# A one-core decoder layer: the first expert pair's token rows are picked by products that hold the one-hot matrix still

## The chip, the cores and the metric

The kernel runs on one core of a Trainium2 chip. The metric is the device time of one execution in microseconds (us). Engines are named as in the profile: PE (TensorE matmul), PEld (its weight load), DVE (VectorE), ACT (ScalarE), POOL (GpSimd) and SP (SyncE, which here only issues DMAs).

## The reference, cut to what matters

One decoder layer on 512 tokens of width 1024 in float32: a token mixer with three branches, then a two-level mixture of experts, then a final RMSNorm. Only the experts matter here. A router gives each token two of 32 experts; each expert is a gated MLP of width 256:

```python
xb = x_pad[toks]                                       # rows of the tokens of one expert
a = jax.nn.silu(xb @ w_gate_e[e]) * (xb @ w_up_e[e])
return a @ w_down_e[e]                                 # then scaled and summed back by token
```

## The kernel before, in words

**Pairs.** The 32 experts are taken as 16 pairs. A pair works on 128 slots, 64 for each of its two experts. Slot-to-token assignment is a one-hot matrix `P` of 512 tokens by 128 slots (`onehot`, L1069, on DVE). `by_slot` (L1074) multiplies it with a few columns on PE, which gives each slot's token number; `place` (L1080, DVE) makes it an index; `fetch` (L1085) issues an indirect gather of 128 rows of 1024 from the copy `xd` in HBM into `self.XG`, on POOL's queue. There are two such buffers: `XG[0]` for even pairs and `XG[1]`, which is a part of the tile `XB`, for odd ones (L995). `turn_x(c)` (L1099) transposes four 128-column blocks of the gathered rows on PE and scales them on ACT. `up(k)` (L1126, `U0` to `U7` in the orders below) multiplies them with one block of gate and up weights for both experts, `turn` (L1137) transposes the result, `down` (L1144, `D`) multiplies it with the down weights. The first nine pairs scatter their result with an accumulating indirect DMA into `xo` in HBM; from then on `xo` is loaded into SBUF (`ACC<-xo`, L1341) and the later pairs are added there by one-hot products (`combine`, L1170).

**The first pair** has no gathered rows. `pick_x(k)` (L1090, `X0` to `X7`) makes the already transposed block k directly: four products over the token tiles, with a block of the token rows `ACC` held in the array and `P` moving.

**Weights.** Each pair has 12 pieces of 512 KB (`w_e`), loaded by SP in a fixed order into a ring of 40 places (L661 to L701). A piece is requested when the piece that held its place before has been multiplied; `used(n)` after every second `up` and after `down` moves that on. SP issues in order: a request whose place isn't free holds back all requests behind it. Pieces 36 to 39 go to the place of `ACC`, the token rows that `pick_x` reads. They are not loaded by `used` but by the step `L` of the order.

**Order.** All engines follow an order that is written out by hand, for pair 0 `SEQ0` (L1276), for the others `SEQM`. `b1` and `b2` are the fetches for pairs 1 and 2, `j` the slot numbers and weights (`info`), `o` a later pair's one-hot matrix, `x0` and `x1` the next pair's `turn_x`, `f` a fetch.

Of the kernel before, what the change touches and what calls it, by code (L numbers as in the profile page):

```python
# [9 lines left out]
F32 = mybir.dt.float32  # L10
# [3 lines left out]
AF = mybir.ActivationFunctionType  # L14
# [23 lines left out]
P_MIX, P_MEM, P_Q, P_KV, P_PS, P_GB, P_FFN, P_END = 0, 8, 16, 19, 21, 25, 49, 57  # L38
# [3 lines left out]
def trunk_and_moe(ctx, tc, a, out):  # L42
    nc = tc.nc
    v, s, g, pe = nc.vector, nc.scalar, nc.gpsimd, nc.tensor
# [34 lines left out]
    def nm(b):  # L79
        n[0] += 1  # L80
        return f"{b}{n[0]}"

    def at(dt=F32, shape=(128, 512)):
        return UA.tile(list(shape), dt, tag="u", name=nm("u"), bufs=8)
# [17 lines left out]
    def mt(dt=F32, shape=(128, 512)):  # L102
        return G2.tile(list(shape), dt, tag="m", name=nm("m"), bufs=6)
# [4 lines left out]
    def bank(p, tag, bufs, shape=(128, 512)):  # L108
        return p.tile(list(shape), F32, tag=tag, name=nm(tag), bufs=bufs)

    def mmb():
        return bank(PA, "mm", 4)

    K = cst.tile([128, C_END], F32, name="K")
    PR = cst.tile([128, P_END], F32, name="PR")
# [223 lines left out]
    ps = mmb()  # L339
# [157 lines left out]
    for h_ in range(XHEADS):  # L497
# [3 lines left out]
        ps = mmb()  # L501
        mm3(ps[:, :MEM], kterms(w, ms))
        tick()
        t = mt()
# [28 lines left out]
    for h_ in range(XHEADS):  # L533
# [22 lines left out]
        ps = mmb()  # L556
        hs = slice(h_ * 128, (h_ + 1) * 128)
# [25 lines left out]
    def swap(src):  # L583
        b = mt()
        for q in range(4):
            o = (q ^ 1) * 32
            s.copy(b[q * 32:(q + 1) * 32], src[o:o + 32])
        return b
# [8 lines left out]
    b = swap(kr)  # L597
# [13 lines left out]
    scale = 192.0 ** -0.5  # L611
# [23 lines left out]
    for d in range(KD):  # L635
        w = WS.use("w_bpm", d)
        res = []
        for j, y in enumerate((yp, ym)):
            ps = mmb()
# [39 lines left out]
    def load_piece(i):  # L679
        e, c = pieces[i]  # L680
        ts = place(i)
        n_ = 2 // len(ts)
        for t in ts:
            if len(ts) == 2:
                t = t.unsqueeze(1)
            sync.dma_start(t, a["w_e"][e, :, c * T:(c + n_) * T].rearrange("p (k f) -> p k f", f=T))
            W[e][c:c + n_] = [t[:, j] for j in range(n_)]
            c += n_
# [12 lines left out]
    def used(n_):  # L701
        ring["used"] += n_
        load(max(min(ring["used"] + RING, 3 * RING - 4), ring["used"] + RING - 4))
# [96 lines left out]
    for h_ in range(HEADS):  # L800
        for op in SEQ:
            k, i = op[0], op[1:]
# [21 lines left out]
            elif k == "V" and h_ % 2:  # L824
                p = (h_ + 1) // 2
# [97 lines left out]
    def row_major():  # L923
        return W1.tile([128, 8, T], F32, tag="ac", name=nm("ACC"), bufs=1).rearrange("p (t a) b -> p t (a b)", t=4).rearrange("p t (a b) -> p t a b", b=128)

    ACC = row_major()
# [65 lines left out]
    def ct2(dt=F32):  # L992
        return C2.tile([128, 1024], dt, tag="y", name=nm("y"), bufs=3)

    XG = [ct2(), XB[:, 0:2].rearrange("p a b -> p (a b)")]  # L995
    g.memset(XG[0], 0.0)
    RR, sm = ct2(), ct2()
    R1, R2 = (RR[:, i * 512:i * 512 + 512].rearrange("p (a b) -> p a b", a=4) for i in range(2))
    L = R1[:, :, 0:36]
# [4 lines left out]
    def bc(x, *shape):  # L1004
        while len(x.shape) < len(shape):
            x = x.unsqueeze(len(x.shape))
        return x.broadcast_to(list(shape))
# [31 lines left out]
    tokr = cst.tile([128, 4, 2], F32R, name="tokr")  # L1039
# [12 lines left out]
    PC = Scope("pc", space=PSUM).p  # L1052
# [8 lines left out]
    def ut(shape, dt=F32):  # L1061
        return W1.tile(list(shape), dt, tag="e1", name=nm("u"), bufs=18) if extra[0] else at(dt, shape)

    class Pair:
# [22 lines left out]
            g.indirect_dma_start(out=self.XG, out_offset=None, in_=xd[:, :], in_offset=bass.IndirectOffsetOnAxis(ap=ix[:, :1], axis=0),  # L1087
                                 bounds_check=T - 1, oob_is_err=False)

        def pick_x(self, k):  # L1090

            if k % 4 == 0:
                self.xps = bank(PC, "xe", 2, (128, 4, 128))
                self.xe.append(ut((128, 4, 128)))
            for t in range(4):
                pe.matmul(self.xps[:, k % 4], lhsT=ACC[:, t, k], rhs=self.P[:, t].bitcast(F32), start=t == 0, stop=t == 3)
            s.activation(self.xe[-1][:, k % 4], self.xps[:, k % 4], AF.Copy, scale=PR[:, P_FFN + k:P_FFN + k + 1])

        def turn_x(self, c):  # L1099
            ps = bank(PC, "xe", 2, (128, 4, 128))  # L1100
# [69 lines left out]
    def combine(i, q):  # L1170
        t, hs = i // 2, slice((i % 2) * 512, (i % 2) * 512 + 512)
        cb = bank(PC, "cb", 1) if i % 2 else bank(PC, "xe", 2)
        for j in range(2):
            pe.matmul(cb, lhsT=q.PT[:, t], rhs=q.y[j][:, hs], start=j == 0, stop=j == 1)  # L1174
        dst = ACC[:, t].rearrange("p a b -> p (a b)")[:, hs]
        v.tensor_tensor(dst, dst, cb, op=OP.add)  # L1176

    def pairs(x):
        return x.rearrange("p t (b a) -> p t a b", b=2)
# [5 lines left out]
    PP = [Pair(p, pairs(code)[:, :, p], None, scattered=p < SC) for p in range(NP)]  # L1185
    for q in PP[:3]:
        q.onehot()


    v.tensor_reduce(sm[:, 6], t4, axis=AX, op=OP.add)  # L1190
    v.scalar_tensor_tensor(sm[:, 9], sm[:, 8], 1.0, sm[:, 6], op0=OP.add, op1=OP.mult)
# [3 lines left out]
    v.tensor_tensor(t32, A1, bc(sm[:, 10], 128, 4, 32), op=OP.mult)  # L1195
    v.tensor_tensor(Wd, A2, bc(sm[:, 11], 128, 4, 32), op=OP.mult)
    v.tensor_tensor(Wd, Wd, t32, op=OP.add)
    tok = K[:, C_TOKID:C_TOKID + 4]
    INF = cst.tile([128, 4, NE // 2, 8], F32R, name="INF")

# [9 lines left out]
    def tiles():  # L1210
        mps = bank(PC, "y", 2, (128, 32))
        for t in range(4):
            pe.matmul(mps, lhsT=KB[:, B_ONES:B_ONES + 128], rhs=Ab[:, t], start=t == 0, stop=t == 3)
        v.reduce_max(nt[:, 0:16], mps.rearrange("p (b a) -> p a b", b=2), axis=AX)
        v.reduce_max(nt[:, 16:17], nt[:, 0:16], axis=AX)
        v.tensor_scalar(flag, nt[:, 16:17], float(CAP), None, op0=OP.is_gt)
# [56 lines left out]

    SEQ0 = "X0 b1 X1 b2 X2 U0 X3 U1 X4 U2 X5 U3 X6 U4 X7 U5 j0 o U6 j1 x0 U7 L x1 j2 j f".split()  # L1276
    SEQM = "o U0 c U1 j c U2 c t c U3 x0 D n U4 w c U5 c x1 c U6 f c U7".split()
    SEQL = "t D U0 U1 U2 U3 U4 U5 U6 U7".split()
    todo = []
# [2 lines left out]
    def wide():  # L1282
        return W0.tile([128, 2, T], F32, tag="e0", name=nm("e"), bufs=6).rearrange("p a b -> p (a b)")

    for p, q in enumerate(PP):
        q.wts = [W[2 * p], W[2 * p + 1]]
        last = p == NP - 1
        if p == NP - 2:
            gf = XG[0]
            g.dma_start(gf, a["final_g"].broadcast_to([128, D]))  # L1290
        if last:
            while todo:
                todo.pop(0)()
            order.__exit__(None, None, None)
            with tc.If(nc.values_load(flag[0:1, 0:1], min_val=0, max_val=1) > 0):
                extra[0] = True
                overflow()
                extra[0] = False
            order = tc.manual_schedule()
            order.__enter__()  # L1300

            q.rw = fs[:, 0, 3:4]
            v.tensor_tensor(q.rw, q.rs, q.wt, op=OP.mult)
        for op in (SEQ0 if p == 0 else SEQL if last else SEQM):
            n_ = int(op[1]) if len(op) > 1 else p + 3
            if op[0] == "U":
                q.up(n_)
                if n_ % 2:
                    used(2)
            elif op == "c" and todo:  # L1310
                todo.pop(0)()
            elif op[0] == "X":
                q.pick_x(n_)
            elif op[0] == "b":
                PP[n_].fetch(PP[n_].by_slot(tokr, 2)[:, 0:1])
            elif op[0] == "x" and not last:
                PP[p + 1].turn_x(n_)
            elif op == "w" and SC <= p < NP - 1:
                q.where()
            elif op == "L":  # L1320
                PP[0].place(PP[0].it[:, 6:7])
                for i in range(RING - 4, RING):
                    load_piece(i)
            elif op == "n" and p == 1:
                tiles()
            elif op[0] in "ojf" and n_ < NP:
                if op[0] == "o":
                    PP[n_].onehot()
                if op[0] == "j":
                    PP[n_].info()  # L1330
                if op[0] == "f":
                    PP[n_].fetch(PP[n_].it[:, 6:7])
            elif op == "t":
                PP[p - 1].turn()
            elif op == "D":
                PP[p - 1].down()
                used(4)
                if p == SC:
                    ACC = row_major()
                    for t in range(4):  # L1340
                        g.dma_start(ACC[:, t].rearrange("p a b -> p (a b)"), xo[t * 128:(t + 1) * 128])  # L1341
                if p > SC:
                    todo += [lambda i=i, q=PP[p - 1]: combine(i, q) for i in range(8)]

    junk, o = wide(), wide()
    hs = [slice(hf * 512, hf * 512 + 512) for hf in range(2)]
    s.activation(fs[:, 4, 0:1], q.a[:, 0:1], AF.Sqrt, scale=0.0)
    ys = [bank(PC, "y", 2) for hf in range(2)]
    for t in range(4):
# [7 lines left out]
        f = fs[:, t]  # L1357
# [9 lines left out]
    f = fs[:, 4]  # L1367
# [103 lines left out]
```

## Time and profile before

| | |
|---|---|
| times of three runs | 804.89, 805.36, 809.42 us (median 805.36) |
| the profiled execution | 807.81 us, of which the span is 806.0 us |
| granted TensorE clock | 0.991 of full speed |
| PE busy | 779.0 us (97%) |
| DVE, ACT, POOL busy | 365.8, 304.4, 276.8 us |
| DMA | 164.17 MB, mean 204 GB/s; weights and other SP and ACT loads 50.3% of the 16 engines' span |

A busy share of PE tells little by itself, since matmuls are pipelined and a slower stream of them still counts as busy. The stage matters: the expert pairs run from 526 us to the end, and there the DMA engines are nearly as full as PE.

### The profile page before, as it was taken

How to read it: one execution, taken by the hardware profiler on the slowest of the kernel's cores; microseconds unless marked ns; L12 is line 12 of the kernel's file. 1: busy time of each engine (PE TensorE's matmuls, PEld its weight loads, DVE VectorE, ACT ScalarE, POOL GpSimd, SP SyncE). 2: the span in 40 equal slices, each digit the busy share in tenths (PEclk: the TensorE clock that was granted, in tenths of full speed). 3: DMA queues.
4: the chain of work that ended last, by engine and by line, in shares of the span. 5: the costliest groups of instructions: out<-in, count | busy, mean ns of one | idle time of the engine just before them, and what ended most of it. 6: DMA issues, size and time to landing. Idle time of an engine off the chain costs nothing. (4 is left out here: it accounts for less than half of the span.)

```text
span 806.0 us, 10157 instructions
## 1 busy us (share of the span) xinstructions
PE 779.0 (97%) x3741; PEld 524.1 (65%) x3743; DVE 365.8 (45%) x675; ACT 304.4 (38%) x626; POOL 276.8 (34%) x169
## 2 busy tenths in 40 slices
PE   7999999999999999999999999999999999999894
PEld 3778888888887888788888888754333333333331
DVE  5668693243455134677774532323121223454424
ACT  6254453343336444655553321213222222222232
POOL 3256677533332688422225644311121212000000
PEclk9999999999999999999999999999999999999988
DMA  6533333321121322111224489979999999999933
GB/s 223 179 105 105 105 105 136 125 105 71 62 92 38 98 95 92 46 47 56 79 87 176 147 313 340 372 257 354 394 370 397 391 374 392 405 354 408 405 125 120
DMA packets 53509, 164.17 MB, mean 204 GB/s; under 512 B 7906, under 2 KB 9058, under 8 KB 53456
## 3 DMA queue, kind: packets, MB, share of 16 engines
q1 hardware_dynamic: 46224, 149.14, 50.3%
q0 software_dynamic: 4640, 9.90, 3.8%
q10 hardware_dynamic: 2592, 4.46, 1.5%
q8 instruction: 30, 0.49, 0.2%
q14 instruction: 23, 0.19, 0.1%
HBM read 158.82 MB, written 11.53 MB: 211 GB/s over the span
## 5 line engine op out<-in xcount | busy, mean ns | idle before, releaser
L125 POOL TENSOR_TENSOR wl<-r,wh 128x1024 fp32r<-128x1024 f32 (+3 forms) x75 | 167.7, 2244 | 210.8 <-ACT wh L180 189.7
L180 ACT CAST wh<-r 128x1024 fp32r<-128x1024 f32 (+3 forms) x85 | 82.1, 972 | 32.0 <-PE mm L199 12.6
L1131 PE MATMUL gu<-e,u 128*64 128x512 f32 x336 | 88.8, 607 | 0.9 <-DMA e<-in_w_e 0.9
L198 PE MATMUL mm<-g,wh 128*128 128x512 f32 x180 | 71.9, 400 | 0.0
L199 PE MATMUL mm<-g,wh 128*128 128x512 f32 x180 | 70.2, 390 | 0.0
L1107 ACT ACTIVATE u<-xe,PR 128x128 f32<-128x128 f32 x120 | 34.2, 367 | 67.4 <-PE xe L1103 67.3
L471 PE MATMUL mm<-box,wh 128*128 128x512 f32 x144 | 56.8, 394 | 0.9 <-ACT wh L180 0.9
L472 PE MATMUL mm<-box,wh 128*128 128x512 f32 x144 | 56.3, 391 | 0.0
L201 PE MATMUL mm<-g,wl 128*128 128x512 f32 x180 | 52.7, 391 | 0.0
L1158 POOL DMA_INDIRECT xo<-y,ix x9 | 14.3, 1594 | 89.9 <-DVE ix L1082 79.7
L435 ACT ACTIVATE m<-s,st 128x256 f32<-128x256 f32 (+3 forms) x48 | 24.3, 508 | 54.4 <-DVE st L433 53.9
L1131 PEld LDWEIGHTS gu<-e,u 128*64 128x64 f32 x336 | 20.4, 135 | 33.0 <-issue 26.1
L1167 PE MATMUL y<-e,u 128*64 128x512 f32 x160 | 38.9, 600 | 0.4 <-DMA e<-in_w_e 0.4
L201 PEld LDWEIGHTS mm<-g,wl 128*128 128x128 f32 x180 | 33.8, 188 | 7.5 <-POOL wl L125 0.2
L198 PEld LDWEIGHTS mm<-g,wh 128*128 128x128 f32 x180 | 34.0, 189 | 6.5
L199 PEld LDWEIGHTS mm<-g,wh 128*128 128x128 f32 x180 | 33.9, 188 | 6.4
L476 PE MATMUL mm<-box,wl 128*128 128x512 f32 x144 | 36.6, 390 | 0.0
L198 PE MATMUL mm<-box,wh 128*128 128x512 f32 x78 | 31.7, 406 | 0.5 <-DVE g L283 0.5
L471 PEld LDWEIGHTS mm<-box,wh 128*128 128x128 f32 x144 | 27.1, 188 | 6.7 <-ACT wh L180 1.3
L1154 DVE TENSOR_SCALAR y<-y,it 128x512 f32<-128x512 f32 x9 | 6.8, 751 | 54.1 <-PE y L1167 54.1
L476 PEld LDWEIGHTS mm<-box,wl 128*128 128x128 f32 x144 | 27.0, 188 | 5.8
L472 PEld LDWEIGHTS mm<-box,wh 128*128 128x128 f32 x144 | 27.1, 188 | 5.3
(358 smaller groups left out, 1657.3 us busy)
## 6 DMA issues: line engine op xcount, KB each, us to landing
e<-in_w_e SPq DMA_DIRECT2D x124, 512.0 KB
r<-in_w_in SPq DMA_DIRECT2D x37, 512.0 KB
r<-in_w_e SPq DMA_DIRECT2D x15, 512.0 KB
wh<-in_w_e SPq DMA_DIRECT2D x15, 512.0 KB
wl<-in_w_e SPq DMA_DIRECT2D x15, 512.0 KB
m<-in_w_e SPq DMA_DIRECT2D x30, 256.0 KB
r<-in_w_bpm SPq DMA_DIRECT2D x8, 512.0 KB
r<-in_w_bl SPq DMA_DIRECT2D x8, 512.0 KB
```

What stands on the lines that cost most here:

```text
L125: eng.tensor_tensor(lo, x, hi.bitcast(F32), op=OP.subtract)
L180: s.copy(hi[:, :cols], r[:, :cols])
L198: pe.matmul(ps, lhsT=lh, rhs=rh, start=start and i == 0, stop=False)
L199: pe.matmul(ps, lhsT=lh, rhs=rl, start=False, stop=False)
L201: pe.matmul(ps, lhsT=ll, rhs=rh, start=False, stop=stop and i == m - 1)
L435: s.activation(P[:, :w], S[:, :w], AF.Exp, bias=st4[:, 0:1], accum_out=st4[:, 1:2])
L471: pe.matmul(ps, lhsT=lh, rhs=rh, start=k == 0, stop=False)
L472: pe.matmul(ps, lhsT=lh, rhs=rl, start=False, stop=False)
L476: pe.matmul(ps, lhsT=ll, rhs=rh, start=False, stop=k == KD - 1)
L1107: s.activation(x[:, j], ps[:, j], AF.Copy, scale=PR[:, k:k + 1])
L1131: pe.matmul(gu[r], lhsT=self.xe[k // 4][:, k % 4, r], rhs=self.wts[b][k], start=k == 0, stop=k == KD - 1)
L1167: pe.matmul(y[r], lhsT=self.aT[:, k, r], rhs=self.wts[b][8 + 2 * k + hf], start=k == 0 and not more, stop=k == 1)
```

## The change

The first pair's rows are no longer made in transposed form. `pick_x(hf)` now holds a tile of the one-hot matrix in the array and moves 512 columns of the token rows, for each half of the width; ACT copies the result into `XG[0]`, and the ordinary `turn_x` transposes it. Both halves stand right behind the first one-hot matrices, ahead of the order `SEQ0`, with pair 1's slot numbers between them. The step `L`, the request for the four pieces in the place of `ACC`, stands behind the first `turn_x` instead of behind `U7`. Pair 0's place index, which stood in `L` too, becomes a step `p` of its own. The fetch for pair 2, which writes `XG[0]`, stands behind `X1`. `XG[0]` is no longer cleared.

```diff
     XG = [ct2(), XB[:, 0:2].rearrange("p a b -> p (a b)")]
-    g.memset(XG[0], 0.0)
...
-        def pick_x(self, k):
-
-            if k % 4 == 0:
-                self.xps = bank(PC, "xe", 2, (128, 4, 128))
-                self.xe.append(ut((128, 4, 128)))
+        def pick_x(self, hf):
+
+            hs = slice(hf * 512, hf * 512 + 512)
+            ps = bank(PC, "y", 2)
             for t in range(4):
-                pe.matmul(self.xps[:, k % 4], lhsT=ACC[:, t, k], rhs=self.P[:, t].bitcast(F32), start=t == 0, stop=t == 3)
-            s.activation(self.xe[-1][:, k % 4], self.xps[:, k % 4], AF.Copy, scale=PR[:, P_FFN + k:P_FFN + k + 1])
+                pe.matmul(ps, lhsT=self.P[:, t].bitcast(F32), rhs=ACC[:, t, 4 * hf:4 * hf + 4].rearrange("p a b -> p (a b)"), start=t == 0, stop=t == 3)
+            s.copy(self.XG[:, hs], ps)
...
+    def first_fetch(p):
+        PP[p].fetch(PP[p].by_slot(tokr, 2)[:, 0:1])
+
+    PP[0].pick_x(0)
+    slot1 = PP[1].by_slot(tokr, 2)
+    PP[0].pick_x(1)
...
     v.tensor_tensor(Wd, Wd, t32, op=OP.add)
+    PP[1].fetch(slot1[:, 0:1])
     tok = K[:, C_TOKID:C_TOKID + 4]
...
-    SEQ0 = "X0 b1 X1 b2 X2 U0 X3 U1 X4 U2 X5 U3 X6 U4 X7 U5 j0 o U6 j1 x0 U7 L x1 j2 j f".split()
+    SEQ0 = "X0 L U0 X1 b2 U1 U2 U3 U4 U5 j0 o U6 j1 x0 U7 p x1 j2 j f".split()
...
             elif op[0] == "X":
-                q.pick_x(n_)
+                q.turn_x(n_)
             elif op[0] == "b":
-                PP[n_].fetch(PP[n_].by_slot(tokr, 2)[:, 0:1])
+                first_fetch(n_)
...
+            elif op == "p":
+                PP[0].place(PP[0].it[:, 6:7])
             elif op == "L":
-                PP[0].place(PP[0].it[:, 6:7])
                 for i in range(RING - 4, RING):
                     load_piece(i)
```

## Rows read from the trace of the kernel before

**Rows 1.** The page's second part: the span in 40 slices of 20.15 us, busy tenths of PE and of the DMA engines, and GB/s.

```profile
PE   7999999999999999999999999999999999999894
...
DMA  6533333321121322111224489979999999999933
GB/s 223 179 105 105 105 105 136 125 105 71 62 92 38 98 95 92 46 47 56 79 87 176 147 313 340 372 257 354 394 370 397 391 374 392 405 354 408 405 125 120
```

**Rows 2.** The busy times by stage: stretch, its length, busy us of PE, PEld, DVE, ACT and POOL with the number of instructions, then granted clock, DMA share and GB/s.

```profile
531.50:534.50 3.00, 3.00 (x18) 1.36 (x16) 0.00 (x0) 0.73 (x2) 1.04 (x1) 1.00 0.55 157
534.50:550.00 15.50, 15.18 (x90) 8.38 (x88) 4.07 (x21) 4.12 (x13) 0.00 (x0) 1.00 0.74 249
550.00:561.00 11.00, 11.00 (x58) 4.01 (x56) 1.77 (x10) 2.94 (x9) 2.61 (x2) 1.00 1.02 373
561.00:594.00 33.00, 32.72 (x158) 11.76 (x156) 6.50 (x22) 9.06 (x27) 6.29 (x5) 1.00 1.03 390
...
700.00:762.50 62.50, 62.07 (x262) 23.01 (x258) 32.17 (x58) 15.80 (x42) 2.54 (x3) 1.00 1.01 391
764.50:771.50 7.00, 6.12 (x16) 1.98 (x18) 0.75 (x1) 1.06 (x2) 0.00 (x0) 0.52 1.00 383
```

**Rows 3.** The waits of SP, the queue that requests the pieces (L686), from 530 to 552 us: who it waited for, us in total, times, longest.

```profile
SPq L686 <- PE gu L1131: 15.3, 5, 5.0
```

**Rows 4.** The same view from 575 to 700 us.

```profile
SPq L686 <- DMA e<-in_w_e: 60.7, 51, 2.2
...
SPq L686 <- PE gu L1131: 2.5, 9, 0.4
```

**Rows 5.** The instructions of PE in order of time, 655 to 705 us. L1140 is a pair's turn, L1167 a down.

```profile
657.26 0.44 PE L1140 MATMUL at<-K,u 128*128 128x128 f32 x2
...
670.43 0.44 PE L1140 MATMUL at<-K,u 128*128 128x128 f32 x2
...
673.66 1.07 PE L1167 MATMUL y<-e,u 128*64 128x512 f32 x2 [0.19 <-DMA e<-in_w_e]
...
682.05 0.73 PE L1174 MATMUL xe<-y,u 128*128 128x512 f32 x2 [0.70 <-DVE ACC L1176]
...
693.63 0.38 PE L1140 MATMUL at<-K,u 128*128 128x128 f32 x2
```

**Rows 6.** The same view, 700 to 806 us.

```profile
712.68 0.38 PE L1140 MATMUL at<-K,u 128*128 128x128 f32 x2
...
730.18 0.38 PE L1140 MATMUL at<-K,u 128*128 128x128 f32 x2
...
781.03 1.98 PE L1356 MATMUL y<-ACC,P 128*128 128x512 f32 x4 [0.60 <-DVE ACC L1176]
```

**Rows 7.** The instructions of PE in order of time, 526 to 549 us (idle time before and its releaser in brackets). L1096 is a pick, L1077 a by_slot, L1131 an up, L1103 a turn_x.

```profile
526.05 1.16 PE L1096 MATMUL xe<-P,ACC 128*128 128x128 f32 x8
526.96 0.58 PE L1077 MATMUL at<-tokr,P 128*128 128x2 f32 x4
...
531.57 1.08 PE L1131 MATMUL gu<-e,u 128*64 128x512 f32 x4
...
533.67 1.08 PE L1131 MATMUL gu<-e,u 128*64 128x512 f32 x4
...
545.08 0.66 PE L1103 MATMUL xe<-K,XB 128*128 128x128 f32 x4
...
548.54 0.65 PE L1131 MATMUL gu<-e,u 128*64 128x512 f32 x2
```

**Rows 8.** All instructions of line L1356, the last pair's product with the one-hot matrix held and the token rows moving: weight loads and passes, ns shortest, median and longest.

```profile
L1356 PEld LDWEIGHTS y<-ACC,P x16: 186/188/190, 781.0 to 791.7; 128*128 128x128 f32 x16
L1356 PE MATMUL y<-ACC,P x16: 592/592/697, 781.0 to 792.1; 128*128 128x512 f32 x16
```

**Rows 9.** Groups of ACT by shape, 505 to 520 us (busy us, mean ns of one), and an ACT row of the order of time.

```profile
L915 ACT COPY ACC<-tr 128x512 f32<-128x512 f32 x2 | 1.2, 585 | 4.7 <-PE tr L911 4.7
...
545.78 1.14 ACT L1107 ACTIVATE u<-xe,PR 128x128 f32<-128x128 f32 x4 [3.24 <-PE xe L1103]
```

**Rows 10.** The gathers: POOL in order of time, 526 to 560 us, and the last line of what the trace says of line L1087 as a whole.

```profile
530.26 1.09 POOL L1087 DMA_INDIRECT XB<-xd,ix  x1 [7.13 <-DVE ix L1082]
531.65 1.04 POOL L1087 DMA_INDIRECT y<-xd,ix  x1 [0.30 <-issue]
...
DMA to landing us min/median/max: 3.3/8.3/15.3
```

**Rows 11.** The instructions of SP in order of time, 527 to 562 us, neighbours merged: start, us from the first's start to the last's end, what, how many.

```profile
534.77 12.80 SPq L686 DMA_DIRECT2D e<-in_w_e  x8
547.80 1.83 SPq L686 DMA_DIRECT2D ac<-in_w_e  x4
```

**Rows 12.** Busy times in stretches of half a microsecond (columns as in rows 2).

```profile
535.00:535.50 0.50, 0.50 (x7) 0.50 (x6) 0.00 (x0) 0.00 (x0) 0.00 (x0) 1.00 0.00 0
535.50:536.00 0.50, 0.50 (x6) 0.34 (x6) 0.00 (x0) 0.13 (x1) 0.00 (x0) 1.00 0.87 123
```

**Rows 13.** The load of the accumulated rows, POOL and DVE in order of time.

```profile
674.10 2.21 POOL L1341 DMA_DIRECT2D ACC<-xo  x4 [8.03 <-DMA e<-in_w_e]
...
681.31 0.69 DVE L1176 TENSOR_TENSOR ACC<-ACC,xe 128x512 f32<-128x512 f32 x1 [1.22 <-DMA ACC<-xo]
```

**Rows 14.** A step of the chain that ended last: start, us, what.

```profile
766.04 6.41 PE y L1167 x16
```

## The prediction

> **What bounds the kernel now.** I read the page's 40 slices first [rows 1]. From slice 24 PE and the DMA engines are both nearly full, except that DMA falls from 372 to 257 GB/s in the slice at 524 to 544 us, the stage of the change. Next the stretches [rows 2]: from 531.5 to 534.5 us DMA moves 157 GB/s, to 550 us 249, then 373, 390 and more at a share of 1.02 to 1.03. So weight pieces come at full rate from 550 us on, with a hole of 18.5 us before. The waits of SP say why. In the hole it waits for PE's ups alone (15.3 us, five times) [rows 3]: each pair of pieces needs a place that two ups free. From 575 to 700 us it waits almost only for earlier DMAs (60.7 us on e alone, 2.5 us on ups) [rows 4].
>
> Who sets the end? A pair without stalls takes PE 13.17 us from turn to turn (657.26 to 670.43), the next one takes 23.2 (to 693.63), with waits for pieces [rows 5]; then 19.05, and 17.5 when nothing stalls and eight combines are in it [rows 6]. The 23.2 us hold seven combines, one of some 0.6 us less, so 16.9 were due: 6.3 us lost, and 1.5 in the next, 7.8 in all. After 700 us PE is busy for 62.07 of 62.5 us [rows 2]. So pieces arrive too slowly for PE until 698 us, PE uses up its lead by 672 us and waits; from there it works without a pause to the end. What DMA delivers earlier before 698 us comes off the end, up to 7.8 us plus what PE gains itself.
>
> **The picks.** Removed are eight picks of 1.16 us each, most of them between ups; a pick and an up together take 2.10 us (531.57 to 533.67) [rows 7]. Added are two half picks, each four float32 products of 512 columns in two passes. The last pair's product has this very shape: one pass lasts 592 ns, a group's first up to 697 [rows 8], and four passes take 1.98 us, so a pass follows the last after (1.98 - 0.70) / 3 = 0.43 us [rows 6]. A half pick is 8 x 0.43 + 0.1 = 3.55 us. The first starts at 526.05 as the pick does now [rows 7] and ends at 529.6, pair 1's by_slot takes 0.5, the second half pick runs from 530.1 to 533.65. ACC is then free.
>
> Each of the 16 loads of the one-hot tile takes 188 ns [rows 8]. Four loads and four passes one behind the other would take L1356 0.75 + 4 x 0.43 + 0.16 = 2.6 us; it took 1.98 [rows 6], so the loads lie beside the passes. [...]
>
> **Turns, copies, small steps.** X0 and X1 are turns of 0.66 us [rows 7]. ACT copies each half in 0.585 us and scales four blocks in 1.14, the first in 0.37 [rows 9]. The copy of the second half stands ahead of X0's scaling: 533.8 to 534.4; U0 starts at 534.9, against 531.57 now. Then X1, b2 and seven ups without picks between (two passes side by side by two, 0.86 us, and some 0.1 where another kind of work stood ahead): U1 ends at 537.8, U3 at 539.5, U5 at 541.3, U7 at 544.6. Pair 1's U0 comes at about 546.8 instead of 548.54 [rows 7]: PE gains 1.7 us.
>
> Pair 1's fetch: its by_slot is done at 530.1, so the gather is issued at about 530.5 against 530.26 [rows 10]. DVE waits there for PE some 1.5 us, and the INF instructions behind it too; their first reader, j0, is at 541, so that is hidden; were it not, 1.5 us. Pair 2's gather moves from 531.65 to about 537.5, with only gathers behind it on POOL; it lands after 8.3 us in the median, 15.3 at worst [rows 10], at 546 to 553, and pair 1's x0 needs it at about 551.6. At worst PE waits a microsecond while it has a lead of tens; nothing. The memset on POOL, the index p and the order on DVE have one answer, nothing.
>
> **The request L.** Now it stands behind U7: four pieces at 547.80, behind eight that trickled out from 534.77 over 12.8 us [rows 11]. After the change SP reaches L first; it needs the place of ACC, free at 533.65. Queued behind it on SP are all further pieces, the first of which needs U1, 537.8, so they lose nothing. Pieces move about 0.75 us after the request: DMA stands still from 535.0 to 535.5 and moves from 535.5 on, after the request at 534.77 [rows 11, 12]. So L moves from 534.5; four pieces of 524 KB at 390 GB/s last 5.4 us, to 539.9. U1 has then freed two more (2.7 us, to 542.6), U3 two (545.3), U5 two (547.9), U7 two (550.6), pair 1's U1 the next at 548.7. The stream doesn't break again.
>
> **The sum.** At 390 GB/s the hole could carry 18.5 x 390 = 7215 KB; it carried 3.0 x 157 + 15.5 x 249 = 4331. Missing are 2884 KB, 7.4 us. What remains is 531.5 to 534.5. If the 471 KB that move there now still do, 1.8 us are missing; if they don't, since pair 2's gather (512 KB) moves out of it into the full stream, 3.0. So DMA is 4.4 to 5.6 us ahead. By shares instead of bytes: (1.03 - 0.55) x 3 + (1.03 - 0.74) x 15.5 = 5.9, 5.8 us at a full share of 1.03, less 3.0: 2.8 us. The share counts a packet that waits as busy and bytes count a small-packet gather as idle; I take 4.0 us, and keep 2.8 and 5.6. Behind 550 us places are freed in time: PE frees them 1.7 us earlier, and some six pieces are on their way by then, 8 us of DMA. PE reaches its starvation 1.7 us earlier, loses 7.8 + 1.7 - 4.0 = 5.5 us instead of 7.8, and everything behind is 4.0 us earlier. Profiled: 807.81 - 4.0 = 803.8 (span 802.0). That execution stood 2.45 us above the median of the runs; from the median 805.36, **801.4 us**.
>
> **Rivals.**
> - *The accumulated rows hold PE.* ACC<-xo is issued at 674.10, behind a scatter that waited 8.03 us, and DVE waits for it at 681.31 [rows 13], PE at 682.05 [rows 5]. It hangs on pair 8's down, which is not starved and gains only PE's 1.7 us. For: the wait exists already. Against: from 682.05 to the turn at 693.63 stand five ups of 0.93, five combines of 0.62 and a by_slot of 0.5, 8.3 us, where 11.6 were spent; 3.3 of the 7.8 us are lost there and 1.5 behind, and can be won there. It would leave 1.7 us: 803.7. Chance 0.14.
> - *Hidden anyway.* The ring's places or the slower gathers give back the gain by 600 us: 805.4. For: SP still waits for ups for 2.5 us between 575 and 700. Against: these waits are of 0.4 us at most, beside 60.7 us for DMAs [rows 4]. Chance 0.10.
> - *More.* The whole hole closes because the first gather fills what remains: 7.4 us, 798.0. The starvation of 7.8 us could carry it. Chance 0.13.
> - *The picks end late.* All of SP's queue stands behind L, so each microsecond that ACC is freed later costs one. It decides at 4 us: L behind 537.7 us is no gain. [...] Chance 0.05.
> - *Loads that aren't hidden.* 16 loads of 0.188 us on the picks' path free ACC at 536.7: a gain of 1.0 us, 804.4. Against: the row of four passes [rows 6]. Chance 0.03. [...]
>
> **How the numbers follow.** The forecast has 0.55, 799.8 to 802.6. The rivals have the rest. The range that leaves out no more than 2 in 10 runs from 798.0 (the end of *more*) to 805.8 (*hidden* with a little noise; the three runs lie 0.5 to 4.5 us apart). One per cent, 8.05 us, is about what a measurement of this kernel can tell from no change, and nearly every case lies inside: 0.05 faster (a part of *more*, with noise), 0.92 within, 0.03 slower (*late*, beyond what is priced).
>
> **What would show it.** In the profile after: two groups of eight passes of about 3.6 us at 526 and 530; four ac pieces requested near 533.7; SP's waits for ups between 530 and 552 down from 15.3 us to few, replaced by waits for DMAs; a DMA share near 1 from 535.5; pair 1's U0 near 546.8; the turns up to the one at 670.43 earlier by 1.7 us, and those from 700 on by 4. It is wrong if ac is requested after 537, if a second hole opens, or if the turns near 690 gain only 1.7 us.

## The result, and the profile after

The changed kernel takes **802.37 us** (median of 20 runs, 800.6 to 804.6); the kernel before, in 20 runs beside them, 807.79 (804.89 to 811.6). The ratio is 0.9931 (0.992 to 0.9943): 5.4 us or 0.7% faster. Forecast were 801.4 us, in 798.0 to 805.8, and a gain of 4.0. The profiled execution took 801.17 us, span 799.4, granted clock 0.995.

The page's slices of 20.0 us first (busy tenths of the DMA engines, GB/s). The slice with the first pair now moves 309 GB/s, 257 before [rows 1]; the two slices don't begin at the same work, so the stretches further below are the better measure.

```profile
DMA  6523334322221323211115479999999999999943
GB/s 218 187 106 106 106 106 132 132 80 80 80 79 44 108 89 82 64 47 57 54 54 211 132 281 339 363 309 392 390 381 388 398 353 399 407 360 403 408 170 121
```

The instructions of PE in order of time, from the first pick on. L1094 is a half pick, L1076 a by_slot, L1101 a turn_x, L1129 an up.

```profile
526.55 3.70 PE L1094 MATMUL y<-ACC,P 128*128 128x512 f32 x8
529.69 0.90 PE L1076 MATMUL at<-tokr,P 128*128 128x2 f32 x4
530.46 3.68 PE L1094 MATMUL y<-ACC,P 128*128 128x512 f32 x8
533.97 0.60 PE L1101 MATMUL xe<-K,y 128*128 128x128 f32 x4
535.08 1.08 PE L1129 MATMUL gu<-e,u 128*64 128x512 f32 x4 [0.51 <-ACT u L1105]
...
546.93 1.94 PE L1129 MATMUL gu<-e,u 128*64 128x512 f32 x8
```

The instructions of SP in order of time, then its waits from 530 to 552 us (us in total, times, longest), then the stretches (columns as in [rows 2]).

```profile
534.20 1.75 SPq L686 DMA_DIRECT2D ac<-in_w_e  x4
538.12 29.37 SPq L686 DMA_DIRECT2D e<-in_w_e  x24
```

```profile
SPq L686 <- PE gu L1129: 11.7, 6, 2.9
SPq L686 <- PE y L1094: 2.8, 1, 2.8
```

```profile
532.00:535.00 3.00, 2.57 (x9) 1.09 (x8) 0.00 (x0) 0.83 (x3) 0.76 (x1) 1.00 0.54 169
535.00:550.50 15.50, 15.10 (x81) 7.05 (x82) 4.78 (x26) 4.61 (x17) 2.03 (x2) 1.00 1.00 360
550.50:561.00 10.50, 10.50 (x54) 3.70 (x55) 1.23 (x5) 3.74 (x11) 2.66 (x2) 1.00 1.03 408
```

The first pair's stage is as the change meant it: two half picks, the four ac pieces requested 13.6 us earlier than in [rows 11], and a DMA share of 1.00 where it was 0.74 [rows 2]. Now follows the place where PE ran out of pieces [rows 5]: rows of PE, POOL and DVE from 662 us on, and all that the trace lists as waits of PE from 650 to 712 us.

```profile
668.82 0.44 PE L1138 MATMUL at<-K,u 128*128 128x128 f32 x2
...
670.79 3.65 PE L1165 MATMUL y<-e,u 128*64 128x512 f32 x16
...
680.48 0.73 PE L1172 MATMUL xe<-y,u 128*128 128x512 f32 x2 [2.41 <-DVE ACC L1174]
...
683.47 2.84 PE L1129 MATMUL gu<-e,u 128*64 128x512 f32 x8
...
687.92 0.61 PE L1076 MATMUL at<-INF,P 128*128 128x8 f32 x4
...
690.61 0.38 PE L1138 MATMUL at<-K,u 128*128 128x128 f32 x2
```

```profile
662.87 1.59 POOL L1156 DMA_INDIRECT xo<-y,ix  x1 [10.19 <-DMA e<-in_w_e]
672.32 2.22 POOL L1348 DMA_DIRECT2D ACC<-xo  x4 [7.86 <-DMA e<-in_w_e]
```

```profile
679.74 0.69 DVE L1174 TENSOR_TENSOR ACC<-ACC,xe 128x512 f32<-128x512 f32 x1 [2.89 <-DMA ACC<-xo]
```

```profile
PE xe L1172 <- DVE ACC L1174: 2.4, 1, 2.4
```

No wait for a piece is listed any more: the down at 670.79 runs in one block, where the one at 673.66 of [rows 5] stopped for its weights. In place of these waits stands one of 2.41 us for the accumulated rows, 0.70 before [rows 5]. Behind it the granted clock falls to 0.50:

```profile
682.00:685.30 3.30, 3.30 (x10) 1.10 (x10) 1.44 (x3) 0.00 (x0) 1.03 (x1) 0.50 1.03 411
```

### The profile page after: what moved, and what is told of

Its sections match the earlier page's. It is cut to its first block, busy times and chain, and to the rows that moved or that the text cites. A ratio compares the mean times of both kernels' runs of the same rounds, so it can differ in the third digit from the quotient of the medians.

```text
span 799.4 us, 10085 instructions
## 1 busy us (share of the span) xinstructions
PE 771.9 (97%) x3703; PEld 520.1 (65%) x3703; DVE 365.8 (46%) x675; ACT 305.0 (38%) x628; POOL 276.1 (35%) x168
## 5 line engine op out<-in xcount | busy, mean ns | idle before, releaser
L1129 PE MATMUL gu<-e,u 128*64 128x512 f32 x336 | 85.6, 613 | 0.5 <-ACT u L1105 0.5
L1105 ACT ACTIVATE u<-xe,PR 128x128 f32<-128x128 f32 x128 | 36.6, 368 | 70.7 <-PE xe L1101 67.3
L1129 PEld LDWEIGHTS gu<-e,u 128*64 128x64 f32 x336 | 20.4, 137 | 33.6 <-issue 30.1
L1165 PE MATMUL y<-e,u 128*64 128x512 f32 x160 | 37.0, 599 | 0.0
```

The lines of the kernel that those rows point to most:

```text
L1105: s.activation(x[:, j], ps[:, j], AF.Copy, scale=PR[:, k:k + 1])
L1129: pe.matmul(gu[r], lhsT=self.xe[k // 4][:, k % 4, r], rhs=self.wts[b][k], start=k == 0, stop=k == KD - 1)
L1165: pe.matmul(y[r], lhsT=self.aT[:, k, r], rhs=self.wts[b][8 + 2 * k + hf], start=k == 0 and not more, stop=k == 1)
```

## The experiments

Absolute times of two executions differ for reasons that have nothing to do with the change: the mixer ends at another time (first picks from 525.65 to 528.48 us in the table below), the full DMA stream is a little faster or slower (352 and 368 GB/s from 650 to 675 us in b0 and in the execution forecast from), the clock falls in the program's last pairs (0.50 from 764.8 to 771.6 us in that execution) or not (1.00 in after). So I read every trace by three lengths worked out from the starts in the order of PE's instructions: **A**, from the first pick to the turn at 670.43 us in [rows 5] (144.38 us there); **B**, from that turn over the next two intervals to the one at 712.68 in [rows 6] (42.25 there; 34.4 without stalls, by the prediction's 16.9 + 17.5, but 35.3 with a term that it left out, see below); **C**, the last interval between two turns. The three intervals between B and C took 52.23 to 52.25 us in every trace.

| kernel | median us | ratio to before | first pick | A | B | C |
|---|---|---|---|---|---|---|
| before, the execution forecast from | 807.79 | | 526.05 | 144.38 | 42.25 | 18.87 |
| b0_before | 806.39 | 0.9978 (0.9955 to 1.0001) | 526.18 | 144.39 | 44.00 | 17.24 |
| b1_before | 809.31 | 1.0023 (0.9997 to 1.0049) | 526.75 | 146.00 | 42.61 | 15.86 |
| e1_request_late | 807.76 | 0.9999 (0.9979 to 1.002) | 526.01 | 142.28 | 44.43 | 18.82 |
| e2_order_alone | 805.82 | 0.9978 (0.9958 to 0.9998) | 526.12 | 145.04 | 41.63 | 17.54 |
| e5_before_less_four | 805.08 | 0.9975 (0.996 to 0.9991) | 525.69 | 144.40 | 40.35 | 17.56 |
| e9_both_before | 804.50 | 0.9968 (0.995 to 0.9987) | 528.13 | 145.97 | 40.03 | 15.85 |
| after | 802.37 | 0.9931 (0.992 to 0.9943) | 526.55 | 142.27 | 40.21 | 15.86 |
| a0_after | 802.33 | 0.9923 (0.9897 to 0.995) | 528.48 | 142.27 | 40.41 | 15.86 |
| e3_combine_late | 801.25 | 0.9918 (0.9886 to 0.995) | 525.65 | 142.27 | 39.81 | 15.86 |
| e4_after_less_four | 802.01 | 0.9938 (0.9915 to 0.9961) | 526.62 | 142.27 | 39.84 | 17.55 |
| e6_split_release | 800.68 | 0.9919 (0.9897 to 0.994) | 526.64 | 142.26 | 40.01 | 17.55 |
| e7_split_and_late | 801.33 | 0.9928 (0.9907 to 0.9949) | 525.68 | 142.26 | 40.34 | 17.55 |
| e8_both_after | 801.78 | 0.9934 (0.9906 to 0.9962) | 528.04 | 142.28 | 39.42 | 15.84 |

The lengths are worked out before the starts are rounded, so they can differ by 0.01 from the rows. Each ratio is to runs of the kernel before on the same chip in the same round, whose medians were 807.72 (a0, e1, e2, e3), 806.96 (e4 to e7), 806.61 (e8, e9) and 807.42 us (b0, b1); between rounds the ratios are to be compared. The kernel before itself came out at 0.9978 and at 1.0023 with eight runs each (b0, b1), so a median that is 0.2% off shows little alone. A is 146 in b1 and e9: in b1 the granted clock stood at 0.50 from 531.5 to 534.5 us, during the picks; that it did so in e9 is inferred from its A alone.

**a0_after** is the changed kernel again, and **b0_before** and **b1_before** the kernel before; their turn comes last.

> The changed kernel again, beside the kernel before on the same chip. Every theory expects the ratio of the first measurement, 0.993 (5.4 us). The theory that the tail's clock is a matter of chance expects the granted clock to differ from run to run between about 0.987 and 0.995, and the runs with the higher clock to be 1.5 to 2 us shorter; if the clock were part of the change, all runs of it would have the higher one.

802.33 us, the same again. From 672 to 698 us, where the wait for the rows stands, PE is idle for 2.83 us. The granted clock differs from run to run as expected: the three runs at 0.992 or more took 800.96 to 801.12 us, the five at 0.991 or less 802.15 to 803.65.

**e1_request_late: the early picks without the early request.**

```diff
-    SEQ0 = "X0 L U0 X1 b2 U1 U2 U3 U4 U5 j0 o U6 j1 x0 U7 p x1 j2 j f".split()
+    SEQ0 = "X0 U0 X1 b2 U1 U2 U3 U4 U5 j0 o U6 j1 x0 U7 L p x1 j2 j f".split()
```

> The changed kernel with the request L back behind U7, nothing else. Theory 'stream' (the gain is that DMA isn't idle before the first ups free places): DMA then stands still from about 534.5 until U1 frees two places at 538.1 and they move at 538.9, 4 us later than now, and nothing behind makes that good; 4 us slower than the changed kernel, about 806.4, level with the kernel before within 1.5 us. Rival 'PE' (the gain is PE's 1.6 us and the denser products): the picks and ups are the same, so the time stays at 802.4.

The whole gain is gone (807.76), within the 1.5 us that the first theory allowed. Stretches, and the wait for a piece that is back:

```profile
535.00:539.00 4.00, 4.00 (x24) 1.83 (x22) 0.16 (x1) 1.41 (x6) 1.03 (x1) 1.00 0.15 23
539.00:550.00 11.00, 10.68 (x60) 5.07 (x56) 4.62 (x25) 2.66 (x9) 0.99 (x1) 1.00 0.98 350
```

```profile
688.59 1.07 PE L1129 MATMUL gu<-e,u 128*64 128x512 f32 x2 [1.45 <-DMA e<-in_w_e]
```

PE is 2.1 us early in A, as in the changed kernel, and B gives 2.2 back. While pieces are late, a faster PE only waits for them sooner.

**e2_order_alone: the early request with the old picks.** All eight old picks stand ahead of the first up, `L` behind them; pair 0's place index is a step `p` of its own here too.

```diff
-    SEQ0 = "X0 b1 X1 b2 X2 U0 X3 U1 X4 U2 X5 U3 X6 U4 X7 U5 j0 o U6 j1 x0 U7 L x1 j2 j f".split()
+    SEQ0 = "X0 b1 X1 X2 X3 X4 X5 X6 X7 L U0 b2 U1 U2 U3 U4 U5 j0 o U6 j1 x0 U7 p x1 j2 j f".split()
```

> The kernel before with its old picks (token rows held, one-hot matrix moving), but all eight picks ahead of U0, the request L right behind X7, and pair 2's fetch behind U0: the order without the new form. Theory 'stream': the picks end at about 526.5 + 8 x 0.97 + 0.5 = 534.8, L is requested at 535.0, 0.8 us behind the changed kernel; U0 follows at once, with no copies and no turn before the ups: 0 to 1 us slower than the changed kernel, 802.5 to 803.5. Rival 'form' (products that hold the one-hot matrix are what gains): no gain, 807 to 808.

A miss for both: 805.82 lies between the two ranges. Picks in a row cost more than picks between ups. PE, then SP:

```profile
529.35 1.16 PE L1096 MATMUL xe<-P,ACC 128*128 128x128 f32 x8 [0.46 <-ACT u L1097]
...
535.09 1.16 PE L1096 MATMUL xe<-P,ACC 128*128 128x128 f32 x8 [0.46 <-ACT u L1097]
536.71 1.16 PE L1096 MATMUL xe<-P,ACC 128*128 128x128 f32 x8 [0.46 <-ACT u L1097]
```

```profile
537.93 1.75 SPq L686 DMA_DIRECT2D ac<-in_w_e  x4
```

A pick comes every 1.62 us (535.09 to 536.71), since most wait 0.46 us for ACT, which scales the block before; between ups that wait was covered (the trace of before lists none ahead of a pick). So `ACC` is free 3.7 us later than in the changed kernel (534.20), and the request, with all of SP's queue behind it, is late by as much. The median is 3.5 us above the changed kernel's, and A and B together are 4.2 us longer than after's, 2.8 of it in A (PE itself is late) and 1.4 in B (the pieces). The sum is near the price that the prediction's fourth rival gave, 1 us for each us that the picks end late, but two thirds of it are PE's own lateness and not the queue's. Against the kernel before, the 1.9 us are not clear of the spread of its own medians (b0 has the same 0.9978), and A + B, 186.67, is that of the execution that I forecast from, 186.63. So the order alone doesn't give the gain: it needs the new form of the picks.

**e4_after_less_four and e5_before_less_four: a faster stream, nothing else.** In both, pieces 36 to 39 aren't loaded; POOL zeroes their place. These four are the whole of pair 2's down weights (two for each of its experts, L657), not half as the expectations say, so pair 2's result is left out of the sum.

```diff
-                    load_piece(i)
+                    e, c = pieces[i]
+                    t = place(i)[0]
+                    g.memset(t, 0.0)
+                    W[e][c:c + 2] = [t[:, 0], t[:, 1]]
```

> The changed kernel without the load of pieces 36 to 39 (half of the down weights of pair 2; their place is set to zero by POOL, so pair 2's result is left out). DMA has 2.1 MB less to move, 5.4 us at 390 GB/s, and is that much further ahead. Theory 'stream, then accumulated rows': the waits for pieces near 690 go, but the wait for the accumulated rows at 680 stays, so only 0.5 to 1.5 us are gained: 801 to 802. If pieces were still all that binds: 5 us, 797.5.

> The kernel before without the load of the same four pieces (the same part is left out). Picks, ups and their order stay as they are. Theory 'stream': 5.4 us less for DMA ahead of the starvation are worth about what the change was, until the wait for the accumulated rows binds: 5 to 6 us faster than the kernel before, 802 to 803. Rival 'PE' (the gain of the change was in the picks and their order): no gain, 807.5.

The changed kernel doesn't mind (802.01, 4.95 us under the kernel before beside it, where a0 was 5.39 under): it isn't pieces that it waits for. The kernel before gains 1.9 us and not 5 to 6, a miss. That median alone is no larger than the spread of b0 and b1, but A + B, 184.74, lies 1.9 us below the lowest of the three traces of before. Its PE, 672 to 698 us:

```profile
672.04 3.65 PE L1167 MATMUL y<-e,u 128*64 128x512 f32 x16
...
681.73 1.07 PE L1174 MATMUL xe<-y,u 128*128 128x512 f32 x2 [2.40 <-DVE ACC L1176]
```

With the pieces out of the way, the accumulated rows hold PE at once, by 2.40 us, as in the changed kernel. B is 40.35, the changed kernel's 40.21; what is left between these two is A, 2.1 us.

**e3_combine_late, e6_split_release, e7_split_and_late, e8_both_after, e9_both_before: what stands behind the rows?** e3 is the changed kernel with the combines of the pair that first reads the rows moved behind more of its ups:

```diff
+    SEQC = "o U0 U1 j U2 t U3 x0 D n U4 w U5 x1 U6 f U7 c c c c".split()
...
-        for op in (SEQ0 if p == 0 else SEQL if last else SEQM):
+        for op in (SEQ0 if p == 0 else SEQL if last else SEQC if p == SC + 1 else SEQM):
```

e6 takes both halves of the picks token tile by token tile, and loads each of the four pieces straight into the part of `ACC` that its tile leaves, so that the first is requested at 531.30. e7 is both edits.

```diff
...
-        def pick_x(self, hf):
+        def pick_x(self, ts):
...
+            for t in ts:
+                if t == 0:
+                    self.xps = [bank(PC, "y", 2) for hf in range(2)]
+                for hf in range(2):
+                    pe.matmul(self.xps[hf], lhsT=self.P[:, t].bitcast(F32), rhs=ACC[:, t, 4 * hf:4 * hf + 4].rearrange("p a b -> p (a b)"), start=t == 0, stop=t == 3)
...
```

> The changed kernel; in pair 10 alone the first four combines stand behind U7 instead of between its ups. In the changed kernel's trace PE waits 2.41 us at 680.5 for DVE, which waits for the load of the accumulated rows, and the granted clock is 0.5 for 3.4 us behind it. Theory 'accumulated rows bind now': the wait and the clock's fall go, 4 us of PE; the pieces become the next bound, and the time falls by 1 to 3 us, to 799.5 to 801.5. Theory 'pieces still bind at pair 10's down': the time falls by less than 1 us. It is slower if the four combines in a row wait for DVE (0.69 us each, about 0.1 us a combine).

> The changed kernel with the picks taken token tile by token tile for both halves at once, and with pieces 36 to 39 loaded into the tile of the token rows itself, so that each of the four is requested as soon as its own token tile has been read: at 528.4 (behind the earlier requests, 530), 530.6, 532.3 and 534 instead of all at 534.2. DMA gains some 2 us more in the hole. Theory 'accumulated rows bind now': 0 to 1 us faster than the changed kernel, 801.3 to 802.3. Theory 'each microsecond of the stream is still worth one': 2 us, 800.3.

> The early requests of the run before and pair 10's late combines together. If the two bounds are one behind the other, as the traces say (late combines alone left waits for pieces of 0.97, 0.54 and 0.22 us at 688 to 692), the gains add up to more than either: 2.5 to 3.5 us faster than the changed kernel, 799 to 800. If something else binds, no more than the late combines alone, 801.2.

Three small differences, of 1.0 to 1.7 us from a0_after, whose intervals overlap with its own; no version is shown to beat the changed kernel. e3's 801.25 lies in the range of its first theory, without being clear of the noise. For e6 and e7 the ratios, 0.9919 and 0.9928 beside a0's 0.9923, leave less still. For e7 that is a miss: the two gains were to add up to 2.5 to 3.5 us. e6 closes the rest of the hole (312 GB/s from 532 to 535 us, 169 above) and B stays 40.01:

```profile
532.00:535.00 3.00, 2.70 (x10) 1.10 (x8) 0.02 (x1) 1.33 (x3) 0.74 (x1) 1.00 0.91 312
```

e3 shortens the wait for the rows, and others come in its place:

```profile
680.66 0.73 PE L1172 MATMUL cb<-y,u 128*128 128x512 f32 x2 [1.36 <-DVE ACC L1174]
...
689.52 0.66 PE L1101 MATMUL xe<-K,y 128*128 128x128 f32 x4 [0.97 <-DMA y<-xd,ix]
...
691.73 1.07 PE L1165 MATMUL y<-e,u 128*64 128x512 f32 x2 [0.54 <-DMA e<-in_w_e]
```

e8 and e9 join the two edits, late combines and four pieces left out, in the changed kernel and in the one before.

> The changed kernel with both of its limits near 680 us moved at once: pieces 36 to 39 are not loaded (their place is zeroed, so half of one pair's down weights is left out of the sum), which brings every later piece about 3 us forward, and in the program of the pair in which the accumulated rows are read the combining steps of the rows stand behind the last up product. Theory 'the later of pieces and accumulated rows sets the end': with both moved, the 2.41 us wait for the rows goes and the pieces that held the late-combine kernel (0.97, 0.54, 0.22 us) do not come back, so it is some 2 us under the changed kernel: 799.5 to 800.7 us against 802.3. Rival 'something else binds at once' (PE's own work, the turns of the next pair): 801.5 to 802.5 us, as the kernel with the pieces alone left out.

> The kernel before with pieces 36 to 39 not loaded (their place is zeroed, so half of one pair's down weights is left out of the sum) and with the combining steps of the accumulated rows behind the last up product. Its first-pair stage is untouched, so PE does not start earlier. With the pieces alone left out it was 1.9 us under before and waited 2.40 us for the accumulated rows. Theory 'the later of the two': with the rows moved as well it gains 1.5 to 2.5 us more: 802.8 to 803.8 us. Rival 'the pieces' places bind there': as with the pieces alone, 804.8 to 805.5 us, with waits for pieces in place of the wait for rows.

e8 lies in its rival's range and e9 0.3 us under its own rival's, well above the 802.8 to 803.8 of the theory; what binds isn't quite what the rivals named. e8's waits of PE from 670 to 712 us:

```profile
PE cb L1172 <- DVE ACC L1174: 1.2, 1, 1.2
PE xe L1101 <- DMA y<-xd,ix: 0.9, 1, 0.9
PE y L1165 <- DMA e<-in_w_e: 0.6, 2, 0.4
```

The accumulated rows, the rows gathered for the next pair and the pieces come due within some 12 us, and moving one or two of them leaves waits for all three, 2.7 us in e8: B is 39.4 to 40.4 in all seven traces of kernels with the changed stage. e8 and e9 differ in the first pair's stage alone, and their medians by 2.7 us, e4 and e5 by 3.1: where pieces hardly set the end, what PE gains there counts in full.

**b0_before, b1_before: how much of the difference is the execution?**

> The kernel before, profiled again, to see what of the difference is the end of the program and not the changed stage. From the first pick to the turn at 764.92 us the profiled execution took 238.87 us, and the interval to the last turn 18.87 us, 3.0 us more than without a fall of the granted clock. Theory 'the fall in the tail is chance': the 238.87 us come again within 0.2 us, and the last interval is another, 15.9 or 17.6 us. Rival 'it belongs to the old order': 18.8 to 18.9 us again.

> The same kernel a third time. Theory 'chance': 238.9 us up to that turn, and a last interval that differs between the three executions. Rival 'it belongs to the old order': 18.8 to 18.9 us each time.

The last interval is chance, as the first theory said (18.87, 17.24, 15.86 us with the same instructions), but the rest does not come again within 0.2 us, a miss: A + B is 186.63, 188.39 and 188.61 us. In b1 the granted clock was 0.50 during the picks (531.5 to 534.5 us). In b0 A is the same to 0.01 us and B is 1.75 longer; PE, and the stretch of each kernel from 650 us on (b0, then the execution that I forecast from):

```profile
674.26 1.07 PE L1167 MATMUL y<-e,u 128*64 128x512 f32 x2 [0.66 <-DMA e<-in_w_e]
...
689.79 1.07 PE L1131 MATMUL gu<-e,u 128*64 128x512 f32 x2 [1.43 <-DMA e<-in_w_e]
```

```profile
650.00:675.00 25.00, 24.11 (x112) 8.33 (x108) 5.69 (x18) 6.94 (x21) 4.54 (x4) 1.00 1.00 352
```

```profile
650.00:675.00 25.00, 24.38 (x116) 8.41 (x114) 5.54 (x18) 6.94 (x21) 5.13 (x5) 1.00 1.01 368
```

The same requests are served at 352 GB/s instead of 368, and a kernel that waits for pieces pays: (368 - 352) x 25 = 400 KB, by estimate about 1 of the 1.75 us at 390 GB/s. The rest is not accounted for.

## Why the prediction was right, and where its sum was off

**The stage, step by step.** A half pick was put at 3.55 us; its rows last 3.70 and 3.68, the last pass's end included, and the turn starts 3.51 us behind the second. `L` was due 7.65 us behind the first pick (526.05 to 533.7) and came 7.65 behind it (526.55 to 534.20). The first up was due at 534.9 and starts at 535.08, pair 1's U0 at 546.8 and starts at 546.93, in an execution whose first pick was itself 0.50 us later; from the first pick PE gains 22.49 - 20.38 = 2.11 us, not 1.7. Not all of it is the form of the picks. In the old order pair 2's by_slot stood close behind pair 1's and waited for DVE to read it:

```profile
530.04 0.61 PE L1077 MATMUL at<-tokr,u 128*128 128x2 f32 x4 [1.21 <-DVE ix L1082]
```

In the changed order this wait of 1.21 us is gone and one of 0.51 us for ACT has come (535.08), so some 0.7 of the 2.11 us are waits that the order took out. The weight loads are hidden: at 190 ns (the median of the 16 of L1094), one behind the other with the passes, the eight in a half pick would add 1.5 us to its 3.70, and `L` would have come 10.65 us behind the first pick, as the rival of loads that aren't hidden had it (536.7), and not 7.65.

**The stream.** It doesn't break from 535 us on, as forecast, at 360 GB/s instead of the 390 assumed. That SP's waits for ups would nearly go was wrong: 11.7 us in six waits. No cost of theirs shows, since the DMA share beside them is 1.00: the pieces requested at `L` and behind it keep DMA full meanwhile. A request queue that waits says nothing until the DMA share beside it is read.

**The sum.** Forecast were 1.7 us up to the turn at 670.43 and 4.0 behind 700. Measured in the two executions with profiles: 1.61 (to 668.82), and 3.65 at the turns from 709.03 on, or 4.15 from the first pick (A + B: 186.63 to 182.48). So for the execution that was read the sum held within 0.2 us, counted from the first pick. Its parts did not. The stream's 4.0 us were chosen between a count of bytes and one of shares, on the ground of what each of them leaves out: no run shows that ground. What the runs show is that the two counts differ: 157 GB/s went with a share of 0.55, by estimate 285 at a share of 1, and 390 with 1.03, by estimate 379 [rows 2]. I took PE's gain as used up by waiting, and all 4.0 us as the stream's, with 5.5 us of waiting for pieces left. In these two executions 2.1 us are in A, where PE alone sets the pace, and 2.0 in B, where the pieces come earlier. The two don't simply add: PE early with the pieces late gives nothing (e1), the pieces early without PE 1.9 us (e5), both 5.4.

The 7.8 us that I counted as lost were too many. Each of the two intervals holds a by_slot (687.92 above), and the interval of 17.5 us that I measured them by holds none; in e4, where no wait is listed behind the turn at 690.79, the second interval takes 17.95. So 35.3 us were due and not 34.4, and 6.9 were lost before. Of the 40.21 - 35.3 = 4.9 us that are still lost, the listed waits are not for pieces: 2.41 are the wait for the rows, some 1.65 (an estimate: half of 3.3 us) the half clock behind it, and 0.8 stay unassigned, 0.5 of them in the second interval (18.42).

**The rival that was half right.** *The accumulated rows hold PE* had the mechanism, and 0.14. Scatter, load and first add all come earlier by about PE's gain, no more: the scatter from 664.48, in the trace of before, to 662.87, 674.10 [rows 13] to 672.32, 681.31 [rows 13] to 679.74. Its price was wrong: I had the rows leave 1.7 us. But 4.4 us of the old waiting lay behind the rows (3.3 as the argument against it said, and 19.05 - 17.95 = 1.1 in the next interval), and of these most went: from the first read of the rows to the next turn it was 11.6 us and is 10.13, 1.65 of it the half clock. *More* (7.4 us by closing the hole) is answered by e6 and e4: of pieces that come earlier than this no gain shows.

**The gain of 5.4 instead of 4.0.** The median stands on executions that I hadn't seen. Over the three traces of before, A + B is 187.9 us in the mean, over the two of after 182.6: 5.3 us. The execution that I read was the one that lost least in B. The starting point was off too, by 2.4 us: the median of three runs was 805.36, that of twenty 807.79. The two errors have opposite sign, so that 801.4 is so near is luck: from 807.8 the forecast gain would give 803.8. The runs of before also spread wider (6.7 us against 4.0 in twenty each), which fits a kernel that waits for DMA becoming one that waits for its own PE; that is argued, not shown.

**Left open.** The profiled difference of 6.6 us in span holds 3.0 us of C. That differs between executions of one kernel, and so is no part of the change that these traces can show; whether the change makes the fall of the clock in C rarer can't be told from so few (C is 15.84 to 15.86 us, in after at a clock of 1.00, in four of seven traces of kernels with the changed stage and in two of the other seven). Over all runs the clock isn't the gain: its mean is 0.992 both in the 20 runs of the changed kernel and in the 25 of the kernel before beside a0.

## What to carry to other kernels

When requests are issued in order, find the one whose place comes free last and ask what else could free it: here a different form of the first pair's products ended their reads of the token rows early, and so let the request of all later pieces go out 13.6 us earlier. Before counting a gain at a starved stretch, list everything that comes due there within the gain's own size, and sort it by what it hangs on (the transfer stream, or the engine's own progress); the gain of one alone ends at the next. And where a kernel waits for a full DMA stream, one execution is not its median: compare lengths inside several traces.

## What the hardware showed

- A pause of PE can cost more than itself. After waits for the rows of 2.40 to 2.47 us (after, e5, e6) the granted clock fell: to 0.50 for 3.4 us in after, with a mean of 0.93 from 672 to 698 us in all three. In a0 and e4, where PE is idle for 2.83 and 2.56 us in that stretch, the mean is 0.93 too. After waits of 1.04 to 1.36 us for the same rows (e7, e3) it is 1.00.
- The same two pauses in the last pairs are followed by different clocks. PE of after, then of before:

```profile
759.12 0.73 PE L1172 MATMUL cb<-y,u 128*128 128x512 f32 x2 [0.70 <-DVE ACC L1174]
761.27 0.41 PE L1138 MATMUL at<-K,u 128*128 128x128 f32 x2 [1.42 <-DVEq L1301]
```

```profile
762.77 0.73 PE L1174 MATMUL cb<-y,u 128*128 128x512 f32 x2 [0.70 <-DVE ACC L1176]
764.92 0.66 PE L1140 MATMUL at<-K,u 128*128 128x128 f32 x2 [1.42 <-DVEq L1295]
```

  Both wait 0.70 and 1.42 us; then after's clock stays at 1.00, and before's stands at 0.50 for 6.8 us (764.8 to 771.6), and its C is 3.0 us longer. In b0 and b1, the kernel before again, C is 17.24 and 15.86 us. What decides it is not shown.
- A full DMA stream isn't the same from execution to execution: 352 and 368 GB/s from 650 to 675 us in the two rows of the kernel before above, at shares of 1.00 and 1.01.
